# Projection weights loaded one chunk earlier, and the experts' input centred right behind its squares

## The chip, the core and the metric

The kernel runs on one NeuronCore of a Trainium2 chip. Its engines work side by side, each in the order of its own program: TensorE (PE; PEld is its weight load), VectorE (DVE), ScalarE (ACT), GpSimd (POOL) and SyncE (SP), which issues most of the transfers (DMA). The metric is device time in microseconds (us) of one execution; less is better.

## What is computed

One layer of a transformer block for 1024 tokens of width 1024 (with 256 context tokens), all in float32: layer norm and modulation, an input projection, two attentions (a latent one, `y_mla`, and a neighbourhood one, `y_na`), their merge, a second norm, and a mixture of 16 experts in which each expert picks its 128 tokens. The change lies in the merge and in what stands between the two norms:

```python
def _merge(y_mla, y_na, gates, w_proj_mla, w_proj_na, w_out):
    g_mla, g_na = jnp.split(gates, 2, axis=-1)
    return (jax.nn.sigmoid(g_mla) * (y_mla @ w_proj_mla) + jax.nn.sigmoid(g_na) * (y_na @ w_proj_na)) @ w_out

def _layer(...):
    ...
    mix = _merge(y_mla, y_na, gates, lp['w_proj_mla'], lp['w_proj_na'], lp['w_out'])
    x_new = _layer_norm(ALPHA * x + g1 * mix, lp['ln1_g'], lp['ln1_b'])
    u2 = _layer_norm(x_new) * (1 + sc2) + sh2
    moe = _expert_choice_ffn(u2, lp['w_router'], lp['w_exp_gate'], lp['w_exp_up'], lp['w_exp_down'])
    x_new = _layer_norm(ALPHA * x_new + g2 * moe, lp['ln2_g'], lp['ln2_b'])
```

The experts choose tokens by the softmax of `u2 @ w_router`, and `u2` is also what they are fed with.

## The kernel before

The order of the work is written out by hand: each engine runs its instructions in the order in which the program emits them, and waits are put in where data or buffers demand them. Float32 matmuls are done in three passes: `split` gives a tensor a high part (ACT, line 86) and a low part (DVE, line 87), and `mm3` multiplies high by high, high by low and low by high (lines 90 to 92).

The **output projections** run in the pool `pj`. `yT` holds both attentions' results, split into `yhl`. The projection's output columns come in 8 chunks of 128 (`m`); each chunk runs twice, for two halves `b` of the tokens, 24 matmuls of 512 columns each time. `wload(m)` asks for the chunk's weights on the SP queue into `raw` (two buffers) and splits them at once into `hl` (two buffers); in the loop it is called for chunk m+1 at the start of chunk m. Behind the matmuls of (m, b), `gates` multiplies the PSUM result by the gates `sg` (DVE, line 1158) and adds the two attentions into `mix` (line 1161). The PSUM tiles (two, of 1024 columns) are used in turn, so the matmuls of (m+1, b) need `gates` of (m, b). At a chunk's end `wos_load(m+1)` loads 128 rows of w_out on SP and multiplies them by `g1b` on DVE (line 1138), and `small[m]` loads some small tensors. So on DVE each chunk emits: the low part of the next chunk's weights, `gates` for b = 0, `gates` for b = 1, the row of w_out. The pairs of `sg` are loaded on SP two halves ahead, into three buffers. Chunk 0's weights are split ahead of the loop, in two halves, between the splits of `yT`; chunk 1's are split behind the splits of (b, s) = (1, 1).

The **router stage** takes the tokens in 8 blocks of 128. In step t, `main(t)` multiplies block t of `mix` by w_out (48 matmuls, line 1238, in two column halves b of 8 contraction chunks kt), and the dictionary `between` puts other work between its matmuls, mostly on block t-1: `route` transposes the normalised block (line 1309) and ACT copies it to `uT` (line 1310), `logits` multiplies it by the router's weights (line 1317), and `softmax` collects and normalises them (lines 1324, 1337 to 1347). `half(t, b)` adds the residual (line 1248) and takes statistics (line 1249). At the end of a step `norms(t)` normalises the block: line 1264 subtracts the mean and multiplies by the gain, POOL computes the reciprocal deviation `lr` (line 99), line 1277 (1269 in block 7) finishes it by halves, and ACT sums the squares about the new mean into the buffer `u2` (line 1280). Then `pre_mix(t+2)` splits the next but one block of `mix` at the start of step t+1. `norms2(t)` turns the block into the experts' input on DVE: line 1296 centres and scales it into `u2`, line 1298 multiplies by the deviation and shifts. It is emitted in step t+1 behind `softmax`, at (b, kt) = (1, 4), and so ahead of `half(t+1, 1)`. Block 7 has no next step: it is routed and finished behind the loop. Loads of expert weights (`load_next`) are issued on SP in some of the steps into a ring of 17 buffers, and the experts follow.

Of the kernel before, what the change touches and what calls it, by code (L numbers as in the profile page):

```python
# [9 lines left out]
F32 = mybir.dt.float32  # L10
# [17 lines left out]
def block_kernel(ctx, tc, a, out, dbg=None):  # L28
# [56 lines left out]
    def split(hi, lo, src, eng=nc.vector):  # L85
        nc.scalar.activation(hi, src, AF.Copy)  # L86
        eng.tensor_tensor(lo, src, hi.bitcast(F32), op=OP.subtract)  # L87
# [922 lines left out]
    with ExitStack() as st:  # L1010
        p = pool(st, "pj")

        def wload(m):
            raw = p.tile([128, 8, 128], F32, name="raw", bufs=2)
            nc.sync.dma_start(raw, a["w_proj"][m])
            hi, lo = hl_parts()
            if m:
                split(hi, lo, raw)
            return (hi, lo, raw) if m == 0 else (hi, lo)

        hi, lo, raw = wload(0)
        nxt = [(hi, lo)]
        yhl = {}
        for b in range(2):
            cols = slice(b * 512, (b + 1) * 512)
            for s in (1, 0):
                if b == 0:
                    ks = slice(4 * s, 4 * s + 4)
                    split(hi[:, ks], lo[:, ks], raw[:, ks])
                if (b, s) == (1, 0):  # L1030
                    last.pop()()
                    banks(2, 1024, 2, 2)
                yhl[s, b] = big_tile(), big_tile()
                for k in range(4):
                    c = 4 * s + k
                    split(yhl[s, b][0][:, k], yhl[s, b][1][:, k], yT[:, c, cols])
                if (b, s) == (1, 1):
                    nxt.append(wload(1))
        if "ym" in dbg:
            nc.sync.dma_start(dbg["ym"], yT[:, 0:4])  # L1040

# [99 lines left out]
        for m in range(8):  # L1141
            hi, lo = nxt.pop(0)
            if 0 < m < 7:
                nxt.append(wload(m + 1))
            for b in range(2):
                cols = slice(b * 512, (b + 1) * 512)
                sg = sgs.pop(0)
                if 2 * m + b + 2 < 16:
                    sgs.append(sg_load(2 * m + b + 2))
                pt = ps_S()  # L1150
                for s in (1, 0):
                    for kt in range(4):
                        k = 4 * s + kt
                        mm3(pt[:, s * 512:(s + 1) * 512], hi[:, k], lo[:, k], yhl[s, b][0][:, kt], yhl[s, b][1][:, kt], kt == 0, kt == 3)

                def gates(m=m, b=b, pt=pt, sg=sg):
                    t = w1p.tile([128, 2, 512], F32, name="t", bufs=2)
                    nc.vector.tensor_tensor(t, pt.rearrange("p (s c) -> p s c", s=2), sg, op=OP.mult)  # L1158
                    for i in range(2):
                        c = slice(i * 256, (i + 1) * 256)  # L1160
                        nc.vector.tensor_tensor(mix[2 * b + i][:, m], t[:, 0, c], t[:, 1, c], op=OP.add)
                if (m, b) == (7, 1):
                    last.append(gates)
                else:
                    gates()
                if (m, b) == (7, 0):
                    for piece in pre_mix(0, 2):
                        piece()
                    wo_split(0, 0)
                    wo_split(0, 1)  # L1170
            if m < 7:
                wos_load(m + 1)
            small[m]()
# [47 lines left out]
    with ExitStack() as st:  # L1221
# [39 lines left out]
        def norms(t):  # L1261
            xt = xts[t]
            mv, r = aggregate(sts.pop(t))
            nc.vector.scalar_tensor_tensor(xt, xt, mv[:, 0:1], l1g, op0=OP.subtract, op1=OP.mult)
            u2s[t] = p.tile([128, D], F32, name="u2", bufs=2)
            if t == 7:
                st = p.tile([128, 2, 6], F32, name="st2", bufs=1)
                for b, c in enumerate((H0, H1)):
                    nc.vector.scalar_tensor_tensor(xt[:, c], xt[:, c], r[:, 0:1], l1b[:, c], op0=OP.mult, op1=OP.add)
                for b, c in enumerate((H0, H1)):  # L1270
                    nc.vector.bn_stats(st[:, b], xt[:, c])
                mv2[t] = aggregate(st)
                compare(5, 7, 0, 6, nc.gpsimd)
                return
            sm = p.tile([128, 4], F32, name="sums", bufs=3)
            for b, c in enumerate((H0, H1)):
                nc.vector.scalar_tensor_tensor(xt[:, c], xt[:, c], r[:, 0:1], l1b[:, c], op0=OP.mult, op1=OP.add,
                                               accum_out=sm[:, b:b + 1])
            nc.vector.tensor_scalar(sm[:, 2:3], sm[:, 0:1], sm[:, 1:2], 1.0 / D, op0=OP.add, op1=OP.mult)
            nc.scalar.activation(u2s[t], xt, AF.Square, scale=-1.0, bias=sm[:, 2:3], accum_out=sm[:, 3:4])  # L1280
            mv2[t], spread2[t] = (sm[:, 2:3], None), sm[:, 3:4]
# [119 lines left out]
        rowload(l1b, a["ln1_b"])  # L1401
        chunks = {0: 2, 1: 2, 3: 1, 5: 1, 7: 1}
        for t in range(8):
            if t < 7:
                pre_mix(t + 1)[0]()
                pre_x(t + 1)
            for _ in range(chunks.get(t, 0)):
                load_next()
            ps = ps_S(), ps_S()
            between = {(1, 1): lambda: half(t, ps, 0)}  # L1410
            if t == 0:
                between[0, 6] = constants
            else:
                between[0, 7] = lambda: route(t - 1, 0)
                between[1, 0] = lambda: route(t - 1, 1)
                between[0, 4] = lambda: deviation(t - 1)
                between[1, 2] = lambda: logits(t - 1)
                between[1, 4] = lambda: (softmax(t - 1), norms2(t - 1))
            if t >= 2:
                between[0, 3] = lambda: store(t - 2, nc.scalar)  # L1420
            if t == 7:
                rows = hl_tile()
                brow, tok = rows[:, :T], rows[:, T:]
                nc.sync.dma_start(tok, a["tokrow"])
                between[0, 1] = lambda: spread(0, 6)
                between[0, 5] = between[0, 6] = load_next
                between[1, 4] = lambda: softmax(t - 1)
                between[1, 5] = lambda: norms2(t - 1)
                between[1, 3] = lambda: [compare(j, 6) for j in range(3)]
                between[1, 6] = load_next  # L1430
                masks = hl_tile().bitcast(BF16).rearrange("p (i c) -> p i c", i=4)
                masks = [masks[:, i] for i in range(4)]
            main(t, ps, between)
            if t == 7:
                while pos[0] < RB - 2:
                    load_next()
            half(t, ps, 1)
            norms(t)
# [519 lines left out]
```

## Time and profile before

| | us |
|---|---|
| median of 3 timed runs | 1803.76 (1801.29 to 1804.3) |
| the profiled execution | 1792.52 |
| its span, first to last instruction | 1790.7 |
| PE busy | 1676.3 (94%) |
| DVE busy | 1174.9 (66%) |
| ACT busy | 928.5 (52%) |
| POOL busy | 591.8 (33%) |
| mean granted TensorE clock | 0.981 of full speed |

All times below are us from the span's start. The output projections run from about 924 to 1025, the router stage from 1026 to about 1165, the experts from there to the end. In a row of the timeline, the bracket at the end says how long the engine stood idle before that instruction and what ended the wait. SPq is the issue of a transfer on SP's queue, not the transfer. A matmul's duration reaches past the start of the next one, since they are pipelined.

### The profile page before, as it was taken

What the parts mean: (1) busy time and instruction counts of PE and PEld (TensorE: products, weight loads), DVE (VectorE), ACT (ScalarE), POOL (GpSimd) and SP (SyncE); (2) the same over time, 40 slices, a digit from 0 to 9 for tenths busy, and PEclk for the clock granted to TensorE, in tenths of its full rate; (3) what the DMA queues carried; (4) which work ended last, traced back from release to release, by engine and by line L of the source; (5) the groups of instructions that cost most, each with busy time, mean ns of one, the idle gap of its engine ahead of it and who ended that gap; (6) DMA issues with size and microseconds to landing.
All of it is one profiled execution on the core that took longest, in us unless ns stands there. A gap on an engine that the chain in (4) does not pass through costs nothing. (4 is left out here: it accounts for less than half of the span.)

```text
span 1790.7 us, 25352 instructions
## 1 busy us (share of the span) xinstructions
PE 1676.3 (94%) x9609; PEld 1337.7 (75%) x9609; DVE 1174.9 (66%) x1860; ACT 928.5 (52%) x1477; POOL 591.8 (33%) x488
## 2 busy tenths in 40 slices
PE   5999998999999999999988999788999999999995
PEld 3778787897877778888867776556878887888872
DVE  5612251203377766766564577887999999999985
ACT  3422222112366667776660222245777777777764
POOL 0334555542144423222000111256334333433135
PEclk8999999999999999999999999899999999999998
DMA  8334646245244311010026444878999999999944
GB/s 329 113 111 144 224 155 205 83 127 155 81 88 89 75 47 41 21 30 12 1 89 201 164 165 153 328 293 291 366 378 381 392 389 367 384 389 392 361 158 188
DMA packets 96890, 356.62 MB, mean 199 GB/s; under 512 B 28368, under 2 KB 36944, under 8 KB 70912
## 3 DMA queue, kind: packets, MB, share of 16 engines
q1 hardware_dynamic: 78032, 285.78, 44.1%
q0 software_dynamic: 11376, 41.42, 7.7%
q10 hardware_dynamic: 7360, 27.81, 4.0%
q8 instruction: 75, 1.23, 0.3%
q14 instruction: 47, 0.39, 0.1%
HBM read 312.85 MB, written 42.12 MB: 198 GB/s over the span
## 5 line engine op out<-in xcount | busy, mean ns | idle before, releaser
L1712 DVE TENSOR_TENSOR hl<-raw,hl 128x1024 fp32r<-128x1024 f32 x177 | 214.5, 1238 | 21.8 <-ACT hl L1711 19.9
L1711 ACT ACTIVATE hl<-raw 128x1024 fp32r<-128x1024 f32 x182 | 187.9, 1057 | 39.6 <-PE pgate L92 19.0
L405 PE MATMUL pS<-uhi,whi 128*128 128x512 f32 (+1 forms) x440 | 131.0, 386 | 2.4 <-DVE stg L492 1.8
L1608 POOL TENSOR_SCALAR oh<-iot,slot 128x128 bf16<-128x128 f32 x112 | 133.0, 1202 | 0.5
L87 DVE TENSOR_TENSOR wlo<-raw,whi 128x1024 fp32r<-128x1024 f32 x25 | 36.5, 1463 | 143.0 <-ACT whi L86 142.9
L405 PE MATMUL pS<-ulo,whi 128*128 128x512 f32 (+1 forms) x440 | 129.1, 382 | 0.0
L405 PE MATMUL pS<-uhi,wlo 128*128 128x512 f32 (+1 forms) x440 | 128.9, 382 | 0.0
L310 POOL TENSOR_TENSOR sb<-qs,sa 128x512 fp32r<-128x512 f32 x28 | 35.9, 1282 | 255.1 <-DVE sa L309 133.8
L1711 ACT ACTIVATE whl<-raw 128x1024 fp32r<-128x1024 f32 x91 | 96.5, 1060 | 39.5 <-PE pgate L92 19.4
L1865 POOL DMA_INDIRECT acc_d<-ye,idx x15 | 35.1, 2341 | 243.5 <-DVE ye L1859 243.5
L1712 DVE TENSOR_TENSOR whl<-raw,whl 128x1024 fp32r<-128x1024 f32 x88 | 108.4, 1232 | 9.2 <-ACT whl L1711 8.1
L1712 DVE TENSOR_TENSOR raw<-raw 128x1024 fp32r<-128x1024 f32 x89 | 108.8, 1222 | 6.2 <-ACT raw L1711 6.2
L1711 ACT ACTIVATE raw<-raw 128x1024 fp32r<-128x1024 f32 x91 | 96.3, 1058 | 19.7 <-PE pup L92 7.2
L380 POOL TENSOR_TENSOR rawm<-rawm,scol 128x1024 f32<-128x1024 f32 x32 | 63.0, 1969 | 127.9 <-DMA rawm<-in_w_mod_dram 127.9
L1238 PE MATMUL pS<-raw,hl 128*128 128x512 f32 x384 | 96.1, 399 | 2.0 <-DVE t L1158 1.1
L886 DVE TENSOR_REDUCE sn<-pS 128x1 f32<-128x1024 f32 x64 | 78.3, 1223 | 27.4 <-PE pS L92 26.7
L405 PEld LDWEIGHTS pS<-uhi,whi 128*128 128x128 f32 x440 | 79.0, 189 | 22.6 <-issue 4.3
L405 PEld LDWEIGHTS pS<-ulo,whi 128*128 128x128 f32 x440 | 80.2, 188 | 16.4
L405 PEld LDWEIGHTS pS<-uhi,wlo 128*128 128x128 f32 x440 | 80.2, 188 | 16.3
L911 ACT ACTIVATE pt<-pT 128x512 f32<-128x512 f32 x128 | 69.5, 595 | 34.3 <-PE pT L900 31.0
L1238 PEld LDWEIGHTS pS<-raw,hl 128*128 128x128 f32 x384 | 69.7, 188 | 17.6 <-ACT cb L1330 1.5
L900 PE MATMUL pT<-ident,pm 128*128 128x128 f32 x542 | 72.2, 273 | 1.3 <-ACT pt L911 1.3
(493 smaller groups left out, 4683.0 us busy)
## 6 DMA issues: line engine op xcount, KB each, us to landing
raw<-in_w_exp_gate_dram SPq DMA_DIRECT2D x64, 1024.0 KB
raw<-in_w_exp_up_dram SPq DMA_DIRECT2D x64, 1024.0 KB
raw<-in_w_exp_down_dram SPq DMA_DIRECT2D x64, 1024.0 KB
rawm<-in_w_mod_dram POOLq DMA_DIRECT2D x32, 512.0 KB, 3.9
raw<-in_w_in_dram SPq DMA_DIRECT2D x25, 512.0 KB
wm<-in_w_mod_dram SPq DMA_DIRECT2D x8, 1024.0 KB
sig_d<-stg ACTq DMA_DIRECT2D x16, 512.0 KB
sg<-sig_d SPq DMA_DIRECT2D x32, 256.0 KB
```

What stands on the lines that cost most here:

```text
L87: eng.tensor_tensor(lo, src, hi.bitcast(F32), op=OP.subtract)
L310: lo_engine[0].tensor_tensor(lo[:, cs], src[p0:p1, cs], hi[p0:p1, cs].bitcast(F32), op=OP.subtract)
L380: nc.gpsimd.tensor_tensor(raw, raw, scol[:, :, 0:1].to_broadcast([128, KT, 128]), op=OP.mult)
L405: nc.tensor.matmul(pt[:, c0:c1], ww[:, kt], uu[:, kt, c0:c1], start=(kt == 0 and k == 0), stop=(kt == KT - 1 and k == 2))
L886: nc.vector.tensor_reduce(sm[:, 0:1], ps, axis=AX.X, op=OP.max)
L900: nc.tensor.transpose(tb[b][:, (k - k0) * 128:(k - k0 + 1) * 128], Pm[n][:, k * 128:(k + 1) * 128], ident)
L911: nc.scalar.activation(dst, src, AF.Copy)
L1238: nc.tensor.matmul(ps[b], x[:, kt], w[:, kt % 4], start=(kt == 0 and k == 0), stop=(kt == 7 and k == 2))
L1608: nc.gpsimd.tensor_scalar(ohb[:, t], iot, slot[:, t, e:e + 1], None, op0=OP.is_equal)
L1711: nc.scalar.activation(w[:, 0], src, AF.Copy)
L1712: lo_on(e, i).tensor_tensor(w[:, 1], src, w[:, 0].bitcast(F32), op=OP.subtract)
L1865: nc.gpsimd.indirect_dma_start(out=acc_d[:, :], out_offset=bass.IndirectOffsetOnAxis(ap=idx[:, :1], axis=0), in_=ye, in_offset=None, compu ...
```

## The change

In the projections, asking for weights and splitting them are now two functions. `wload()` asks for the next chunk's weights on SP, `wsplit(m)` splits those of chunk m. Two chunks are asked for ahead of everything, the third behind the split of chunk 1, and the one of chunk m+2 at the start of chunk m, just ahead of the split of chunk m+1. The buffers are the same two. In the router stage the two operations of `norms2(t-1)` are taken apart: the first is emitted at the very start of step t, ahead of `pre_mix(t+1)`, the second stays where both stood. In block 7 the subtraction of `norms` is done by halves, each directly ahead of its own half of the next operation. No arithmetic is added or left out.

```diff
-        def wload(m):
-            raw = p.tile([128, 8, 128], F32, name="raw", bufs=2)
-            nc.sync.dma_start(raw, a["w_proj"][m])
+        wraw = []
+
+        def wload():
+            m = len(wraw)
+            if m < 8:
+                wraw.append(p.tile([128, 8, 128], F32, name="raw", bufs=2))
+                nc.sync.dma_start(wraw[m], a["w_proj"][m])
+
+        def wsplit(m):
             hi, lo = hl_parts()
-            if m:
-                split(hi, lo, raw)
-            return (hi, lo, raw) if m == 0 else (hi, lo)
-
-        hi, lo, raw = wload(0)
+            split(hi, lo, wraw[m])
+            return hi, lo
+
+        for _ in range(2):
+            wload()
+        raw = wraw[0]
+        hi, lo = hl_parts()
...
                 if (b, s) == (1, 1):
-                    nxt.append(wload(1))
+                    nxt.append(wsplit(1))
+                    wload()
...
             if 0 < m < 7:
-                nxt.append(wload(m + 1))
+                wload()
+                nxt.append(wsplit(m + 1))
...
             mv, r = aggregate(sts.pop(t))
-            nc.vector.scalar_tensor_tensor(xt, xt, mv[:, 0:1], l1g, op0=OP.subtract, op1=OP.mult)
             u2s[t] = p.tile([128, D], F32, name="u2", bufs=2)
             if t == 7:
                 st = p.tile([128, 2, 6], F32, name="st2", bufs=1)
                 for b, c in enumerate((H0, H1)):
+                    nc.vector.scalar_tensor_tensor(xt[:, c], xt[:, c], mv[:, 0:1], l1g[:, c], op0=OP.subtract, op1=OP.mult)
                     nc.vector.scalar_tensor_tensor(xt[:, c], xt[:, c], r[:, 0:1], l1b[:, c], op0=OP.mult, op1=OP.add)
...
+            nc.vector.scalar_tensor_tensor(xt, xt, mv[:, 0:1], l1g, op0=OP.subtract, op1=OP.mult)
...
         for t in range(8):
+            if t:
+                norms2(t - 1, 0)
...
-                between[1, 4] = lambda: (softmax(t - 1), norms2(t - 1))
+                between[1, 4] = lambda: (softmax(t - 1), norms2(t - 1, 1))
...
-                between[1, 5] = lambda: norms2(t - 1)
+                between[1, 5] = lambda: norms2(t - 1, 1)
```

The SP queue at the head of the projections, before. `raw` is a chunk's weights, `g1b` the gain of w_out, `sg` the gates; the brackets name what the issue waits for:

```order
L1015 DMA raw_8647<-in_w_proj_dram 128x1024 [waits PE_49,Activation_49,Pool_49]
L1015 DMA raw_8684<-in_w_proj_dram 128x1024
L993 DMA g1b_8740<-mod_d_65 128x1024 [waits DVE_49,Activation_49,Pool_49]
L1087 DMA sg_8743<-sig_d_59 128x512 [waits DMAHW7_49,DVE_49,Activation_49]
L1088 DMA sg_8743<-sig_d_59 128x512 [waits DMAHW0_49]
L1087 DMA sg_8746<-sig_d_59 128x512 [waits DMAHW1_49,DVE_49,PE_49]
L1088 DMA sg_8746<-sig_d_59 128x512 [waits DMAHW2_49]
L1137 DMA wos_8742<-in_w_out_dram 128x1024 [waits DMAHW3_49,Activation_49]
```

and now:

```order
L1019 DMA raw_8647<-in_w_proj_dram 128x1024 [waits PE_49,Activation_49,Pool_49]
L1019 DMA raw_8649<-in_w_proj_dram 128x1024
L1019 DMA raw_8689<-in_w_proj_dram 128x1024 [waits DMAHW4_49,DVE_49]
L993 DMA g1b_8742<-mod_d_65 128x1024 [waits DMAHW7_49,Pool_49]
L1096 DMA sg_8745<-sig_d_59 128x512 [waits DMAHW0_49]
L1097 DMA sg_8745<-sig_d_59 128x512 [waits DMAHW1_49]
L1096 DMA sg_8748<-sig_d_59 128x512 [waits DMAHW2_49,PE_49]
L1097 DMA sg_8748<-sig_d_59 128x512 [waits DMAHW3_49]
L1146 DMA wos_8744<-in_w_out_dram 128x1024
```

The third load of weights now stands ahead of `g1b` and of all that follows on SP, and it waits for DVE, which must have split the first chunk out of the buffer that both use.

The DVE in router step 2, from behind block 1's norms to the residual of block 2's second half, before (`hl` is the split of `mix`, `u_...` the experts' input, `lt` the logits):

```order
L87 TENSOR_TENSOR hl<-raw,hl 128x1024
L1287 TENSOR_SCALAR v_9601<-sums 128x1
L1248 SCALAR_TENSOR_TENSOR xt<-xt,pS 128x512
L1249 BN_STATS st<-xt 128x6
L1337 SCALAR_TENSOR_TENSOR lt<-cb,sums,pY 128x16
L1338 SCALAR_TENSOR_TENSOR lt<-lt,r_9603,cb 128x16
L1339 TENSOR_REDUCE sm<-lt 128x1
L1346 RECIPROCAL sm<-sm 128x1
L1347 TENSOR_SCALAR vals<-ex,sm 128x16
L1296 SCALAR_TENSOR_TENSOR u_9574<-xt,sums,sc2b 128x1024
L1298 SCALAR_TENSOR_TENSOR u_9574<-u_9574,r_9603,sh2b 128x1024
L1248 SCALAR_TENSOR_TENSOR xt<-xt,pS 128x512
```

and now:

```order
L1307 SCALAR_TENSOR_TENSOR u_9573<-xt,sums,sc2b 128x1024
L87 TENSOR_TENSOR hl<-raw,hl 128x1024
L1298 TENSOR_SCALAR v_9602<-sums 128x1
L1258 SCALAR_TENSOR_TENSOR xt<-xt,pS 128x512
L1259 BN_STATS st<-xt 128x6
L1348 SCALAR_TENSOR_TENSOR lt<-cb,sums,pY 128x16
L1349 SCALAR_TENSOR_TENSOR lt<-lt,r_9604,cb 128x16
L1350 TENSOR_REDUCE sm<-lt 128x1
L1357 RECIPROCAL sm<-sm 128x1
L1358 TENSOR_SCALAR vals<-ex,sm 128x16
L1309 SCALAR_TENSOR_TENSOR u_9573<-u_9573,r_9604,sh2b 128x1024
L1258 SCALAR_TENSOR_TENSOR xt<-xt,pS 128x512
```

The first of the two operations on `u_...` has moved from behind the softmax to ahead of the split of `mix`; the second alone is left ahead of the residual of the second half.

The DVE on block 7, behind the loop's last matmuls, now. Before, line 1264 did the first operation at full width, 1024 columns, ahead of both halves of the second:

```order
L1263 BN_AGGR mv<-st 128x2
L97 TENSOR_SCALAR lv<-mv 128x1
L1278 SCALAR_TENSOR_TENSOR xt<-xt,mv,ye 128x512
L1279 SCALAR_TENSOR_TENSOR xt<-xt,lr,l1b 128x512
L1278 SCALAR_TENSOR_TENSOR xt<-xt,mv,ye 128x512
L1279 SCALAR_TENSOR_TENSOR xt<-xt,lr,l1b 128x512
L1281 BN_STATS st_10315<-xt 128x6 x2
```

The first operation on the second half of the columns now stands behind the second operation on the first half.

## Rows read from the trace of the kernel before

**Rows 1.** Busy by stretch: us, PE PEld DVE ACT POOL, PEclk, DMA share, GB/s.

```profile
937.96:1014.71 76.75, 68.56 (x289) 54.76 (x289) 37.77 (x49) 6.99 (x7) 10.43 (x15) 0.98 0.59 190
...
1060.52:1075.21 14.69, 13.31 (x78) 10.17 (x76) 10.58 (x21) 3.84 (x9) 2.00 (x2) 1.00 0.30 109
...
1320.00:1360.00 40.00, 40.00 (x188) 32.02 (x187) 37.76 (x40) 31.54 (x35) 14.09 (x11) 1.00 1.00 389
...
912.60:918.80 6.20, 4.36 (x36) 3.11 (x36) 2.28 (x9) 4.39 (x10) 0.00 (x0) 1.00 0.93 336
...
923.20:929.20 6.00, 5.11 (x20) 3.68 (x21) 5.96 (x10) 6.00 (x13) 0.00 (x0) 1.00 0.74 261
```

**Rows 2.** The timeline, PE, around the second chunk of the projections.

```profile
951.57 0.47 PE L90 MATMUL pS<-raw,hl 128*128 128x512 f32 x1 [2.42 <-DVE t L1158]
...
952.34 0.39 PE L90 MATMUL pS<-raw,hl 128*128 128x512 f32 x1
...
962.31 0.39 PE L92 MATMUL pS<-raw,hl 128*128 128x512 f32 x1
```

**Rows 3.** The timeline, ACT and DVE, over the same chunk.

```profile
947.97 1.06 ACT L86 ACTIVATE hl<-raw 128x1024 fp32r<-128x1024 f32 x1 [14.08 <-DMA raw<-in_w_proj_dram]
...
949.06 1.23 DVE L87 TENSOR_TENSOR hl<-raw,hl 128x1024 fp32r<-128x1024 f32 x1 [3.65 <-ACT hl L86]
...
950.21 1.22 DVE L1158 TENSOR_TENSOR t<-pS,sg 128x1024 f32<-128x1024 f32 x1
...
957.61 1.22 DVE L1138 TENSOR_TENSOR wos<-wos,g1b 128x1024 f32<-128x1024 f32 x1 [3.46 <-DMA wos<-in_w_out_dram]
```

**Rows 4.** The timeline, PE, in router step 3.

```profile
1073.70 0.63 PE L1309 MATMUL pT<-ident,xt 128*128 128x128 f32 x4 [0.93 <-DVE xt L1277]
...
1077.23 0.91 PE L1317 MATMUL pY<-uT,wr 128*32 128x128 f32 x16 [0.38 <-ACT uT L1310]
```

**Rows 5.** Timeline, DVE and ACT, router steps 2, 3, then DVE, step 7.

```profile
1066.80 1.28 DVE L1296 SCALAR_TENSOR_TENSOR u<-xt,sums,sc2b 128x1024 f32<-128x1024 f32 x1
...
1068.12 1.28 DVE L1298 SCALAR_TENSOR_TENSOR u<-u,r,sh2b 128x1024 f32<-128x1024 f32 x1
...
1069.32 0.68 DVE L1248 SCALAR_TENSOR_TENSOR xt<-xt,pS 128x512 f32<-128x512 f32 x1
...
1074.51 1.15 ACT L1280 ACTIVATE u<-xt,sums 128x1024 f32<-128x1024 f32 x1 [8.09 <-DVE sums L1279]
...
1076.73 1.23 DVE L87 TENSOR_TENSOR hl<-raw,hl 128x1024 fp32r<-128x1024 f32 x1 [2.26 <-ACT hl L86]
...
1079.90 0.23 DVE L1337 SCALAR_TENSOR_TENSOR lt<-cb,sums,pY 128x16 f32<-128x16 f32 x1 [0.55 <-PE pY L1324]
...
1134.53 0.15 DVE L1287 TENSOR_SCALAR v<-sums 128x1 f32<-128x1 f32 x1 [1.31 <-ACT u L1280]
```

**Rows 6.** The timeline, SP's queue and DVE, head of the projections.

```profile
911.80 0.83 SPq L1015 DMA_DIRECT2D raw<-in_w_proj_dram  x2
...
926.26 0.68 DVE L87 TENSOR_TENSOR hl<-raw,hl 128x512 fp32r<-128x512 f32 x1
...
935.56 1.21 DVE L1138 TENSOR_TENSOR wos<-wos,g1b 128x1024 f32<-128x1024 f32 x1
...
952.29 0.44 SPq L1137 DMA_DIRECT2D wos<-in_w_out_dram  x1
```

**Rows 7.** The timeline, DVE and PE, from chunk 7 into the router stage.

```profile
1022.59 1.22 DVE L1158 TENSOR_TENSOR t<-pS,sg 128x1024 f32<-128x1024 f32 x1
...
1034.10 10.48 PE L1238 MATMUL pS<-raw,hl 128*128 128x512 f32 x45 [1.14 <-DVE t L1158]
```

**Rows 8.** The timeline, DVE and PE, block 7 behind the loop.

```profile
1146.30 1.42 DVE L1269 SCALAR_TENSOR_TENSOR xt<-xt,lr,l1b 128x512 f32<-128x512 f32 x2 [0.44 <-POOL lr L99]
...
1147.20 1.94 PE L1309 MATMUL pT<-ident,xt 128*128 128x128 f32 x8 [4.65 <-DVE xt L1269]
```

**Rows 9.** Waits in the projections: who, for whom: total, times, longest.

```profile
DVE wos L1138 <- DMA wos<-in_w_out_dram: 26.6, 7, 4.3
```


## The prediction

> **What bounds the kernel now.** I read the page first. TensorE (PE) is busy 94% of the span, so most of the time has no pause to take out. Then the busy time by stretch. In the experts, 1320 to 1360 us for one stretch of many, PE is busy without a break at the full clock while DMA moves 389 GB/s [rows 1]. The two stretches that the change touches are different.
>
> *Output projections, chunks 1 to 6.* They take 76.75 us, and PE is busy for only 68.56 of them [rows 1]. Inside a chunk matmuls start 0.2266 us apart: 44 of them between 952.34 and 962.31 [rows 2]. So the 6 x 48 = 288 matmuls need 65.3 us, and 11.5 us are lost. The timeline says where. The matmul at 951.57 is the first of a chunk; PE had stood idle for 2.42 us before it, until VectorE (DVE) line 1158 [rows 2]. That instruction multiplies the first half's result by the gates and so frees the PSUM bank. It could have run long before, since its 24 matmuls, the first of them at 937.96, had ended near 943.7. But DVE takes its work in order, and the low part of the next chunk's weights (line 87, 949.06) stands ahead of it. That one waits for ScalarE (ACT) at 947.97, and ACT for the weights' transfer, which was asked for only one chunk before [rows 3]. So a transfer that PE does not yet need holds up PE through DVE's order.
>
> *Router stage.* Step t projects 128 tokens and, in between, routes token block t-1. It takes 14.69 us [rows 1]. PE waits 0.93 us for DVE line 1277 (the normalised block that it is to transpose) and 0.38 us for ACT line 1310 (the copy of the transposes) [rows 4]. Line 1277 is late because the second half's residual (line 1248 at 1069.32) comes on DVE behind the two full-width operations of `norms2` (1066.80 and 1068.12). Meanwhile DVE had stood idle 2.26 us earlier in the same step, at 1076.73, behind ACT's squares [rows 5].
>
> **The change part by part.**
>
> *Weights one chunk sooner: a gain of 11.5 us.* At the top of chunk m the weights of chunk m+1 have now landed in the chunk before. ACT splits them as soon as chunk m-1's matmuls release the buffer. On DVE the row of w_out (line 1138) still comes first, then the split, then the gates. With its input there the split follows line 1138 directly, and what paces line 1138 is that SP asks for its row only behind the gates of the chunk before. That loop is: gates' end at 951.43, w_out asked for at 952.29 (0.86), used at 957.61 (5.32), then 1.15 to the split, 1.15 to the gates, 1.22 for the gates [rows 3, 6]. That is 9.70 us. PE needs 48 x 0.2266 = 10.88, so PE sets the pace and the pauses go. What is late next is the row of w_out, with 1.2 us to spare.
>
> *Chunk 7 and the way into the router stage: 2.2 us.* From 1014.71 to 1034.10 it takes 19.39 us now. In chunk 7 the gates of the first half start at 1022.59, 7.9 us into the chunk, since the last row of w_out came late too; with that row asked for half a chunk earlier they start when their 24 matmuls end, 23 x 0.2266 + 0.39 + 0.1 = 5.7 us in. From there to PE's first matmul of the second half at 1034.10 it is 11.51 us of DVE work in unbroken order [rows 7]. New: 5.7 + 11.5 = 17.2.
>
> *The price: the SyncE (SP) queue waits earlier, -1.0 us.* The third weight tile shares the first one's buffer, so its load waits on SP until DVE has split the first, at 926.26 + 0.68 = 926.95 us. Behind it stand the loads of `g1b`, two pairs of `sg`, the first row of w_out and a third pair. `g1b` is asked for right behind the two weight tiles of 911.80 now; it goes to about 927.4. DVE wants `g1b` and w_out at 935.56 [rows 6]. Five tiles of 0.524 MB must land by then. Two bursts of the kernel before give the bounds. One (two weight tiles, `g1b`, a pair) was asked for from 911.80, began to flow some 0.8 us later and moved at 336 GB/s; the other (a pair, w_out, a pair) moved at 261 GB/s [rows 1, 6]. At the first rate the five tiles are there at 927.0 + 0.8 + 7.8 = 935.6 (nothing lost), at the second at 937.9 (2.4 us lost). The first three of them are of the fast burst's kinds, the last two of the slow one's: 0.8 + 4.7 + 4.0 makes 936.5, and 1.0 us lost. DVE stands there before the gates of chunk 0, so PE's chunk 1 starts that much later; nothing gives it back.
>
> The Trainium skill speaks against this part here, on its page "DMA: Bandwidth & Descriptors", section "Anatomy of one DMA": a semaphore is waited for by the issuing sequencer, so one waiting load holds all loads behind it. The same section puts a transfer at about 2.0 us plus its bytes over 436 GB/s; as an estimate, five tiles would be there 8.0 us after 927.0, at 935.0, and the price would be nil, the sum 1.0 us better. The two bursts of this trace moved more slowly than that, so they decide.
>
> *`norms2`'s first operation right behind the squares: 7.7 us.* 1.32 us of DVE work (1066.80 to 1068.12) leaves the way to line 1248 and goes into the idle 2.26 us. There it runs after ACT's squares (1074.51 plus 1.15 and 0.19 for reading the sum), so it ends at about 1077.1 and the split of the mix behind it starts 0.3 to 0.4 us later than now [rows 5]. Its cover is the wait for `collect` before line 1337, 0.55 us; if that is gone, `lt` is late by the rest. New loop by the rows: 2.79 from `lt` to line 1248, 5.19 on to the squares, 2.72 to the logits, 2.67 to the next `lt`: 13.37 us, as much as PE's own work (14.69 - 0.93 - 0.38 = 13.38) [rows 4, 5]. So both waits go and nothing new binds, with hardly a margin. Step 2 gains 0.92 (its logits wait belongs to step 1, where nothing is earlier yet), steps 3 to 6 gain 1.28 each, the logits of step 6 another 0.38: 6.4 us. In step 6 line 1248 runs 1.3 us earlier on top, and block 6's squares are 7.7 us earlier than now. Step 7 is DVE's alone from its first instruction behind those squares (1134.53) to its last; there the moved operation only changes its place, so 7.7 passes through.
>
> *Block 7 centred by halves: -0.4 us.* Now one full-width subtraction (1.28) runs while POOL works out `lr`, and then two halves follow at 1146.30 (1.42 for both). In the new order DVE waits for `lr` after half a subtraction and does the other 0.68 us after it. The first half is ready as before, the second 0.68 later. The 8 transposes start at 1147.20 and the second four need it only 1 us in, so some 0.3 of it is hidden [rows 8]. Bounds: 0 and 0.7.
>
> *What follows.* The expert stage starts that much earlier with the same requests released by the same instructions, and PE is busy in all of the stretch shown [rows 1]: the shift reaches the end whole.
>
> **Sum:** 11.5 + 2.2 - 1.0 + 7.7 - 0.4 = 20.0 us. The profiled execution took 1792.5 (span 1790.7), so 1772.5 for one like it. The median shown is 1803.76, 11.2 above the profiled one; no row says why. I take the same 20.0 off it: **1783.8**. Bounds of the terms: price 0 to 2.4, last block 0 to 0.7, and half-clock stretches such as the one that leaves the mean at 0.98 in [rows 1], which may be more in other runs and go with the pauses: 1778 to 1787.
>
> **The rivals.**
>
> *The row of w_out becomes the bound.* If with the other traffic it takes 7.5 us instead of 5.32, the loop is 11.9 and six chunks lose 6 us again: 1789.8. For it: DVE waits for that transfer in every chunk (7 waits, 26.6 us [rows 9]). Against: the longest wait is 4.3 us where the one of my loop is 3.46 [rows 3, 9], which makes the longest landing 6.2 and that loop 10.6, still under 10.88. 13%.
>
> *The moved operation only fills DVE.* If line 1337 comes 0.6 us late in each step, about half of the router's 7.3 is left: 1787.4. For it: the margins above are near nil. Against: DVE is busy 10.58 us of a step [rows 1]. 8%.
>
> *The experts give it back.* DMA moves 389 GB/s without a pause there [rows 1]; if the weights' stream is what really sets the end and it starts only half as much earlier, 10 us stay: 1793.8. Against: PE has no pause there that a late transfer could have made. 5%.
>
> *Nothing moves:* PE's pauses stay, because the gates stand behind w_out as they stood behind the weights: 1803. 2%.
>
> *Slower.* The same row of w_out at the head of DVE, but taking 11 us: the loop is 15.4, against the 12.8 that a chunk takes now, so the projections lose 15.5; chunk 7's 2.2 goes, and the price of 1.0 and the router's 7.3 remain: 9.2 us more, 1813. It decides from a landing of 9.5 us on, where a chunk of 13.8 has eaten the other terms. 2%.
>
> **How the numbers follow.** Forecast 70% (1778 to 1787). To hold the time 8 times in 10 the range goes up over the first two rivals and one us down: 1777 to 1791. A measurement of this kernel tells about 0.2%, 3.6 us, from no change. Faster 0.96 (forecast and the first three rivals), same 0.02, slower 0.02.
>
> **What would show it.** Right: PE starts chunk 7 about 65.5 us after chunk 1 and has no pause over 0.3 us in between; line 87 no longer stands between w_out and a late gate; `g1b` is asked for near 927.4; router steps of 13.4 us without a wait at the transposes; the second four transposes of block 7 half a us later. Wrong: pauses in the projections ended by w_out's transfer, steps over 13.8 us, DMA waits among the experts, or chunk 1 starting over 2.5 us later than now.

## The result, and the profile after

| | before | after |
|---|---|---|
| median on record | 1804.03 us (4 runs, 1801.29 to 1804.55) | 1775.85 us (4 runs, 1770.9 to 1776.61) |
| a second series of runs | 1797.93 (21 runs, 1786.67 to 1803.15) | 1773.4 (6 runs, 1768.3 to 1781.09) |
| span of the first and of a second profiled execution | 1790.7, 1796.1 | 1774.8, 1773.1 |

The ratio on record is 0.9866, with a 95% interval of 0.9832 to 0.9900; in the second series it is 0.9879 (0.9845 to 0.9913). The change is faster: by some 22 to 24 us by these ratios, by 28.2 and 24.5 us by the medians. The forecast was 1783.8 us (1777 to 1791), 20.0 us off a median of 1803.76. So the direction held. The measured median, 1775.85, lies 1.2 us under the lower end of the range; the ratio, taken off the same 1803.76, gives 1779.6, inside it.

The stages first, by busy time in the kernel after (columns as in [rows 1]: length, then PE, PEld, DVE, ACT, POOL, PEclk, DMA share, GB/s). The first line is projection chunks 1 to 6, the second a router step:

```profile
939.72:1005.13 65.41, 65.41 (x288) 54.18 (x289) 38.25 (x50) 5.32 (x5) 9.94 (x15) 1.00 0.69 225
1045.97:1059.41 13.44, 13.14 (x76) 10.27 (x75) 10.56 (x22) 3.84 (x8) 2.01 (x2) 1.00 0.33 119
```

Six chunks take 65.41 us with PE busy in all of them, at the full clock; before they took 76.75, of which 68.56 busy, at a mean clock of 0.98 [rows 1]. A router step takes 13.44 us instead of 14.69.

The timeline of the kernel after at the head of the projections (SP's queue, DVE, PE), then in a router step, then at block 7:

```profile
912.36 15.50 SPq L1019 DMA_DIRECT2D raw<-in_w_proj_dram  x3
927.96 0.38 SPq L993 DMA_DIRECT2D g1b<-mod_d  x1
937.31 1.23 DVE L1147 TENSOR_TENSOR wos<-wos,g1b 128x1024 f32<-128x1024 f32 x1 [1.11 <-DMA wos<-in_w_out_dram]
939.72 0.50 PE L90 MATMUL pS<-raw,hl 128*128 128x512 f32 x1 [2.50 <-DVE t L1168]
...
1048.03 1.28 DVE L1307 SCALAR_TENSOR_TENSOR u<-xt,sums,sc2b 128x1024 f32<-128x1024 f32 x1 [1.31 <-ACT u L1291]
1059.56 0.60 PE L1320 MATMUL pT<-ident,xt 128*128 128x128 f32 x4
...
1125.35 0.92 POOL L99 TENSOR_TENSOR lr<-lv,mhalf 128x1 f32<-128x1 f32 x1 [8.12 <-DVE lv L97]
1128.65 1.09 PE L1320 MATMUL pT<-ident,xt 128*128 128x128 f32 x4 [0.41 <-DVE xt L1279]
1130.28 0.55 POOL L99 TENSOR_TENSOR lr<-lv,mhalf 128x1 f32<-128x1 f32 x1 [4.01 <-DVE lv L97]
```

The row of the three loads of weights lasts 15.50 us, since the third of them waits on SP; `g1b` is asked for at 927.96 instead of behind the two loads of 911.80, and DVE stands 1.11 us before the first row of w_out [rows 6]. The moved operation (L1307) starts right behind ACT's squares, and the transposes that waited 0.93 us [rows 4] wait no more. The second four transposes of block 7 wait 0.41 us.

Stage lengths, each the difference of two row starts, but for the end of the last stage. A: PE's first projection matmul; B: DVE's first row of w_out; C: the gates of (7,1); D, E, F: the first, seventh and eighth `lt`; G: `idx`, expert 0's list of tokens, by which POOL gathers them; H: PE's transpose of `top`, the highest affinities that DVE picks out next for the other experts; End: the end of PE's last instruction. C to D is 17.8 us in all four.

| us | A-B | B-C | D-E | E-F | F-G | G-H | H-End |
|---|---|---|---|---|---|---|---|
| before, first trace | 11.77 | 97.18 | 88.21 | 12.79 | 11.06 | 28.01 | 584.28 |
| before, second trace | 11.78 | 98.78 | 88.19 | 12.79 | 10.83 | 33.65 | 584.91 |
| after, first trace | 12.97 | 83.61 | 81.88 | 11.53 | 11.06 | 31.65 | 584.21 |
| after, second trace | 12.85 | 85.23 | 81.91 | 11.54 | 10.28 | 29.68 | 584.26 |
| mean change | +1.1 | -13.6 | -6.3 | -1.3 | -0.3 | -0.2 | -0.4 |
| forecast | +1.0 | -13.7 | -6.4 | -0.9 | 0 | 0 | 0 |

Up to G the stages together are 20.3 us shorter in the mean, against a forecast of 20.0. From B to C each kernel differs by 1.6 us between its two executions. In the second trace of after this is a stretch of half clock at the start of chunk 1 (columns as above):

```profile
939.03:943.01 3.98, 3.98 (x10) 3.12 (x11) 2.64 (x5) 0.00 (x0) 0.00 (x0) 0.57 0.64 145
```

The granted clock was 0.57 there, behind a pause of PE of 1.86 us, and most matmuls started 0.427 us apart instead of 0.2266. In the first trace of after chunk 1 stands behind a longer pause, 2.50 us, and no such stretch follows. The chunks behind it run without a pause in both traces. From G to H each kernel differs from one execution to the next by more than in any other stage. The experiments are mostly about that place, where the first trace of after lost 3.6 us against the first of before, and the second trace of before 5.6 us.

### The profile page after: what moved, and what is told of

The parts are those of the page before. It is cut to its first block, busy times and chain, and to the rows that moved or that the text cites. A ratio compares the mean times of both kernels' runs of the same rounds, so it can differ in the third digit from the quotient of the medians.

```text
span 1774.8 us, 25355 instructions
## 1 busy us (share of the span) xinstructions
PE 1672.5 (94%) x9609; PEld 1338.5 (75%) x9609; DVE 1174.4 (66%) x1861; ACT 929.4 (52%) x1477; POOL 593.7 (33%) x488
## 4 chain that ended last, share of the span: by engine, by line
PE 69%; DVE 9%; DMA 6%; POOL 6%; ACT 5%; issue 3%; SPq 0%; ACTq 0%; POOLq 0%; DVEq 0%
PE pS L405 10%; PE pY L923 4%; DMA rawm<-in_w_mod_dram 4%; PE pT L900 3%; PE pgate L90 3%; PE pS L90 3%; PE pD L90 3%; PE pS L92 3%; PE pD L92 3%; PE pD L91 3%; PE pup L90 3%; PE pS L91 3%; PE pgate L92 3%; PE pup L91 3%; PE pup L92 3%
```

## The experiments

Every run was timed in rounds beside the kernel before; ratios are to those runs.

**Both kernels again.** No edit.

> The kernel before, unchanged, to see why its profiled execution (1792.5 us) was 11.2 us below the median of its runs. If executions of one kernel scatter by what a single place does, the new trace shows that place: all steps up to the gather of expert 0 as in the first trace (gather issued at 1163.0 +- 1 us from the span's start) and the difference behind it, or a lower granted clock in one stretch. If the first trace comes from a chip that is faster as a whole, every stage is longer by the same 0.6%. Time: 1801 to 1805 in both cases.

Measured: median 1799.07 (12 runs, 1790.21 to 1805.81), ratio 1.0012 (0.9990 to 1.0034). One kernel spreads over 16 us. The new trace reaches `idx` 0.9 us sooner than the first one and PE's transpose of `top` 4.7 us later. Its timeline there (DVE, POOL, PE):

```profile
1163.21 7.02 DVE L1477 TENSOR_TENSOR gg<-picked 128x1 f32<-128x1 f32 x1
1163.25 2.36 POOL L1712 TENSOR_TENSOR whl<-raw,whl 128x1024 fp32r<-128x1024 f32 x1
1165.56 4.64 POOL L1712 TENSOR_TENSOR hl<-raw,hl 128x1024 fp32r<-128x1024 f32 x2
1170.15 0.68 DVE L1525 MAX8 top<-oh 32x8 f32<-32x512 f32 x1
1195.33 0.28 PE L1536 MATMUL pT<-ident,top 32*128 32x32 f32 x1 [5.28 <-DVE top L1525]
```

The same rows in the first trace of the kernel before:

```profile
1164.12 0.16 DVE L1477 TENSOR_TENSOR gg<-picked 128x1 f32<-128x1 f32 x1
1164.30 2.36 POOL L1712 TENSOR_TENSOR whl<-raw,whl 128x1024 fp32r<-128x1024 f32 x1 [0.18 <-ACT whl L1711]
1190.60 0.25 PE L1536 MATMUL pT<-ident,top 32*128 32x32 f32 x1
```

`gg`, the sum of two 128x1 columns that hold the gates of expert 0, takes 0.16 us when POOL's first weight split starts 0.18 behind it, and 7.02 when it starts 0.04 behind it: it ends with POOL's third split, at 1170.20. DVE's search for the highest affinities (`top`) stands behind it, and PE finds it 5.28 us late. So the first expectation, one place that scatters, held; the chip-wide 0.6% fell. With 5.6 us this place accounts for half of the 11.2 us between the first profiled execution and the median; the other half stays open.

> The changed kernel, unchanged, on the chip of the runs beside it, for a second trace. If the loss at the gather of expert 0 is a property of the kernel, the gather again takes about 8 us from issue to the transposes and block 7's store again ends behind the index; if it was a chance of that one execution, the transposes start 4.8 to 5.3 us after the index and the span is about 4 us shorter (1771).

Measured: median 1773.4 (6 runs), ratio 0.9879. The loss at the gather came again, smaller, between what the two expectations said: 6.61 us from issue to transposes, where the first trace had 8.15.

**`gg` with one operand**, on the kernel before:

```diff
-            nc.vector.tensor_tensor(dst, picked[:, i:i + 1], picked[:, i + 1:i + 2], op=OP.add)
+            if i:
+                nc.vector.tensor_reduce(dst, picked[:, i:i + 2], axis=AX.X, op=OP.add)
+            else:
+                nc.vector.tensor_tensor(dst, picked[:, i:i + 1], picked[:, i + 1:i + 2], op=OP.add)
```

> The kernel before with one instruction replaced: the sum of expert 0's gates (gg, two columns of picked) is a reduction of one operand instead of an addition of two; same arithmetic. In the trace of before_again this 128x1 addition took 7.02 us instead of 0.16, from 0.04 us ahead of POOL's first weight split to the end of POOL's third, and PE met the delay at the transposes of top (5.28 us). Theory that DVE's second input and POOL share a port: gg takes 0.2 us or less in this trace, PE waits under 0.5 us at the transposes of top, the median is 2 to 5 us under that of the kernel before and the highest runs (1803 to 1806) become rare. Rival, that DVE was held by something else (its semaphores, the transfers): gg again long in about half of the traces, median equal within 1 us.

Measured: median 1792.71 (11 runs, 1789.91 to 1796.7) against 1798.54, ratio 0.9975 (0.9956 to 0.9995). Nothing is left above 1797, where the 15 runs of the kernel before beside it reach 1805.55. Its timeline:

```profile
1162.81 0.15 DVE L1478 TENSOR_REDUCE gg<-picked 128x1 f32<-128x2 f32 x1
1162.85 2.37 POOL L1715 TENSOR_TENSOR whl<-raw,whl 128x1024 fp32r<-128x1024 f32 x1
1188.83 0.25 PE L1539 MATMUL pT<-ident,top 32*128 32x32 f32 x1
```

POOL starts 0.04 us behind `gg`, as in the bad execution, and `gg` takes 0.15. Over all 14 traces: with two operands and POOL 0.04 behind, `gg` was held in 4 of 4 (7.02 three times, 2.42 once, until POOL's first split ended); with POOL 0.18 or more behind, in 0 of 6; with one operand and POOL 0.04 behind, in 0 of 3 (in the fourth with one operand POOL came later). The Trainium skill states the cause on its page "SBUF — State Buffer", section "Who interferes with whom": a DVE instruction with two inputs in SBUF shares the second read interface with a GpSimd instruction that reads SBUF, and the one issued second waits until the first has ended. The traces agree on which form waits. They differ in two things: the wait lasted over three POOL instructions, 7.02 us, not one of 2.36, in three of the four; and the instruction that was held is, by the trace, the one that started first, by 0.04 us.

**One part alone.** The weights one chunk sooner, with the rest as before; then the moved operation alone, with block 7 by full width (the diffs are the parts of the change).

> Only the weights asked for one chunk sooner; norms2 and block 7 as before. The forecast's terms make 11.5 + 2.2 - 1.0 = 12.7 us less than the kernel before (ratio 0.9930). In the trace: no pause of PE between chunk 1 and chunk 7, the gates of (7,1) 12.4 to 13 us sooner, router steps of 14.7 us as before. If the part of the gain that was lost at the gather of expert 0 in the changed kernel belongs to this part, the time is only 8 to 9 us less, with the gather landing 8 us after its issue instead of 4.8.

> Only the first operation of norms2 moved behind the squares; weights as before, block 7 by full width as before. The forecast's term is 7.7 us less than the kernel before (ratio 0.9957): steps of 13.4 instead of 14.7 us, the logits of block 7 7.5 to 7.9 us sooner. If the shift is lost at the gather of expert 0 (the landing 8 us instead of 4.8), 3.5 to 4.5 us less. If the moved operation only fills DVE (rival of the prediction), 3.6 us less and steps of 14.1.

Measured: weights alone 1781.22 (7 runs), ratio 0.9917 (0.9888 to 0.9947); router alone 1786.85 (9 runs), ratio 0.9942 (0.9919 to 0.9966). Both gained more than their terms in time (about 15 and 10 us for 12.7 and 7.7), but not in their stages. Weights alone: A to C 98.06 us, 10.9 and 12.5 less than in the two traces of before, with 1.6 us lost at half clock in chunk 1 as in the second trace of after. Its trace has a `gg` of 7.02 us and belongs to a run of 1789.63; one other run took 1791.02, and five lie at 1777.85 to 1781.37. Router alone: D to E 81.94 and E to F 11.46, together 7.6 less; its `gg` took 0.16, with POOL 0.74 behind it. That the rest of the gain is a `gg` that is held less often is likely by how the runs fall into groups, but not shown: each kernel has one trace. The two traces also tell which part turns the order at the gather: with the weights alone it follows `idx` by 0.45 us and PE has the rows 4.69 us later; with the router part alone it is 0.67 and 5.26. The full-width block 7 of router alone also prices the halves: 11.46 against 11.53 us, 0.07.

**The split behind the gates**, on the kernel before: the transfer where it was, only DVE's and ACT's split moved.

```diff
             if 0 < m < 7:
-                nxt.append(wload(m + 1))
+                raw = p.tile([128, 8, 128], F32, name="raw", bufs=2)
+                nc.sync.dma_start(raw, a["w_proj"][m + 1])
...
                     gates()
+                if b == 0 and 0 < m < 7:
+                    nxt.append(hl_parts())
+                    split(*nxt[-1], raw)
```

> The kernel before, with the next chunk's weights asked for where they were, but split behind the gates of the first half instead of ahead of them, from chunk 1 on; nothing else changed. Theory of the prediction, that it is DVE's order and not the transfer that stops PE: by the rows of before the low part is ready some 10.2 us into a chunk of 10.88, so the pauses go without an earlier load and without the later g1b: from the first row of w_out to the gates of (7,1) 85 to 88 us on DVE instead of 97 to 99, the first row of w_out 11.8 us behind PE's first projection matmul as before, time 10 to 13 us under the kernel before. Rival, that the weights' transfer is the bound: PE waits for the low part at each chunk's start instead, 2 us or more, and 0 to 5 us are gained.

Measured: B to C 87.7 us, 1785.12 (7 runs), ratio 0.9919 (0.9888 to 0.9950), with a `gg` of 7.02 in its trace. After the first matmul of chunk 1, PE pauses only where chunk 2 begins:

```profile
954.27 0.50 PE L90 MATMUL pS<-raw,hl 128*128 128x512 f32 x1 [1.30 <-ACT hl L86]
955.53 0.50 PE L92 MATMUL pS<-raw,hl 128*128 128x512 f32 x1 [0.53 <-DVE hl L87]
```

So the pauses of the kernel before were made by the split's place on DVE. With the transfer at its old place all but one of them go, and the first row of w_out is not late (A to B 11.77).

**Every row of w_out but the first loaded twice**, on the kernel after.

```diff
             nc.sync.dma_start(wos[:, m], a["w_out"][m * 128:(m + 1) * 128])
+            if m:
+                nc.sync.dma_start(wos[:, m], a["w_out"][m * 128:(m + 1) * 128])
```

> The changed kernel with every row of w_out but the first loaded twice, the second transfer behind the landing of the first. It prices the loop that the prediction found next (gates' end, issue, landing, 1.15 to the gates: 9.70 us, 5.32 of it the landing). Theory: the second landing adds 2.5 to 5.3 us to the loop, which makes 12.2 to 15.0 us a chunk instead of 10.88 or less; seven rows, so 9 to 29 us more than the changed kernel, with DVE waiting for the transfer ahead of every gates of a first half. If the row has more room than that loop says, under 3 us more.

Measured: 1791.13 (9 runs), 16.9 us over the kernel after with one operand, timed beside it; B to C is 102.71 us, against 83.64 there. The shortest turn of the loop that holds all its parts (DVE, PE, SP):

```profile
951.95 1.22 DVE L1170 TENSOR_TENSOR t<-pS,sg 128x1024 f32<-128x1024 f32 x1
953.31 0.47 PE L90 MATMUL pS<-raw,hl 128*128 128x512 f32 x1 [3.61 <-DVE t L1170]
954.03 0.43 SPq L1146 DMA_DIRECT2D wos<-in_w_out_dram  x1
958.63 0.33 SPq L1148 DMA_DIRECT2D wos<-in_w_out_dram  x1
962.09 1.23 DVE L1149 TENSOR_TENSOR wos<-wos,g1b 128x1024 f32<-128x1024 f32 x1 [6.21 <-DMA wos<-in_w_out_dram]
964.37 1.22 DVE L1170 TENSOR_TENSOR t<-pS,sg 128x1024 f32<-128x1024 f32 x1
```

From gates to gates this turn is 12.42 us, and PE stops for 3.61 again. Its landings take 4.60 and 3.46 us instead of one of 5.32, and 9.70 + 2.74 is 12.44. The six turns up to chunk 6 take 12.42 to 14.70 us with landings of 8.06 to 10.33 together, each 4.4 more than its landings, as in the prediction's loop (9.70 - 5.32). So that loop is right. Its spare time shows in the first trace of after itself: until the gates of the first halves have caught up with PE, they follow each other in 9.45 to 10.51 us (chunks 0 to 5), 0.4 to 1.4 less than the 10.88 that PE needs.

**What holds up expert 0.** The chain of waits of the kernel after runs through two transfers, block 7's store and the gather (start, us, what):

```profile
1134.50 9.68 DMA acc_d<-xt
1144.18 8.01 DMA xe<-u_d,idx
1152.33 1.09 PE pY L1656 x4
```

Its timeline (DVE, POOL, SP, PE) shows the order behind it:

```profile
1143.19 0.16 DVE L1490 TENSOR_TENSOR idx<-picked 128x1 int32<-128x1 f32 x1
1144.18 1.09 POOL L1495 DMA_INDIRECT xe<-u_d,idx  x1 [6.81 <-DVE uT L1488]
1144.84 0.33 SPq L1228 DMA_DIRECT2D raw<-in_w_exp_up_dram  x1
1152.33 1.09 PE L1656 MATMUL pY<-ident,xe 128*128 128x128 f32 x4 [9.08 <-DMA xe<-u_d,idx]
```

The first of three 1 MB loads is asked for 1.65 us behind `idx`, in this and in the first trace of before (1164.23 - 1162.58). The gather follows `idx` by 0.45 us there and by 0.99 here, because the store had not landed: so the chain has it, though the row's own bracket names a DVE operation. So the loads come 0.66 us behind the gather instead of 1.19. A load of weights now stands nearer ahead of the store. These are the last such load and the store, before and then after:

```profile
1143.15 0.33 SPq L1218 DMA_DIRECT2D raw<-in_w_exp_gate_dram  x1
1153.90 0.50 SPq L1259 DMA_DIRECT2D acc_d<-xt  x1
```

```profile
1127.59 0.33 SPq L1228 DMA_DIRECT2D raw<-in_w_exp_gate_dram  x1
1134.50 0.44 SPq L1269 DMA_DIRECT2D acc_d<-xt  x1
```

That is 10.75 us ahead and now 6.91; with the weights alone it is 11.43, with the router part alone 6.79. So the nearer load comes from the shorter router steps. Whether it makes the store late is what the first of two edits asks; the second moves the loads behind the gather:

```diff
-                while pos[0] < RB - 2:
+                while pos[0] < RB - 4:
...
         store(7, nc.sync)
+        while pos[0] < RB - 2:
+            load_next()
```

> The changed kernel with the last two expert-weight loads of step 7 issued on SP behind block 7's store instead of ahead of it. In the changed kernel the store, issued at 1134.12 and 1134.50, ended at 1144.18, behind weights that keep DMA at over 400 GB/s to 1139, and the gather of expert 0 and ACT's first weight split waited for it. Theory that the store is what is late: it ends 3 to 5 us earlier, the gather is issued 0.45 us behind idx instead of 0.99, ACT's split starts 0.4 us behind idx. Then POOL's first split comes within 0.2 us of gg, and by the port theory gg takes 7 us in some executions: time between 1772 and 1779, no gain that can be relied on. Rival, that only the three loads behind the gather matter: gather and time as in the changed kernel (1773 to 1776).

```diff
-        load_next()
-        load_next()
-        load_next()
...
         xT = [transposed(xe0, "x", h, True) for h in range(2)]
+        for _ in range(4):
+            load_next(nc.scalar)
```

(with the load inside the first weight splits held back to the same place.)

> The changed kernel with the four expert-weight loads that follow the gather of expert 0 on SP (three of them 0.66 to 1.63 us behind it) issued by ACT behind the copies of expert 0's transposes. Theory that these 1 MB loads hold up the gather: from issue to PE's transposes 4 to 5 us instead of 6.6 to 8.1, tau0's transposes of top 2 to 3.5 us earlier behind idx, time 2 to 3 us under the changed kernel. Rival, that block 7's store alone holds it up: 6.6 to 8.1 us from issue to transposes as before, time equal, or up to 1.5 us more for ACT's issues.

Measured, the gather's issue and the transposes in the kernel with the store ahead, then in the one with the loads behind (its first load goes out at 1150.69):

```profile
1142.55 1.09 POOL L1497 DMA_INDIRECT xe<-u_d,idx  x1 [6.26 <-DMA raw<-in_w_exp_gate_dram]
1143.74 0.33 SPq L1228 DMA_DIRECT2D raw<-in_w_exp_up_dram  x1
1147.67 1.09 PE L1658 MATMUL pY<-ident,xe 128*128 128x128 f32 x4 [5.51 <-DMA xe<-u_d,idx]
```

```profile
1144.16 1.09 POOL L1495 DMA_INDIRECT xe<-u_d,idx  x1 [5.91 <-DMA acc_d<-xt]
1150.69 0.34 ACTq L1228 DMA_DIRECT2D raw<-in_w_exp_up_dram  x1
1148.70 1.09 PE L1653 MATMUL pY<-ident,xe 128*128 128x128 f32 x4 [5.49 <-DMA xe<-u_d,idx]
```

Both cure it: 5.12 and 4.54 us instead of 8.15. With the store ahead of the last two loads the gather also follows `idx` by 0.45 us again, here and in the two later kernels that have it; in the five traces of the kernel after and its variants without it, it is 0.45 (twice), 0.55, 0.73 and 0.99. So it is the loads ahead of the store that can make it late. From idx to PE's transpose of `top` it is 28.22 and 28.78 us. In time they cannot be told from the kernel after: 1774.15 (1772.15, 1774.15 and 1783.96) and 1772.61 (3 runs each).

**Versions meant to be faster than both.**

> The changed kernel with gg as a reduction of one operand, nothing else. In both traces of the changed kernel POOL's first weight split comes 0.8 to 1.1 us behind gg, since ACT's split waits for block 7's store, so by the port theory it meets the long gg seldom: median within 1.5 us of the changed kernel (1773 to 1776), and its highest runs (1780 to 1781) gone if they were such executions. Rival, that the long gg is as frequent here as in the kernel before: 3 to 6 us under the changed kernel.

> The changed kernel with four edits together: gg as a reduction of one operand, block 7's store ahead of the last two weight loads, the four weight loads behind the transposes, and the third projection weight tile asked for behind the first row of w_out instead of ahead of g1b. By the terms measured so far: 1.2 us at the head of the projections, 0.5 at the gather's issue, 2 to 3 at its landing, and no execution with a gg of 7 us: 3.5 to 5 us under the changed kernel, about 1769. If the edits only move waits to the next transfer, within 1 us of the changed kernel.

> The changed kernel with three edits: gg as a reduction of one operand, block 7's store ahead of the last two weight loads of step 7, the third projection weight tile asked for behind the first row of w_out. The loads behind the gather stay on SP. By the traces so far: 1.1 us at the head, 1.5 to 3.4 us from idx to the transposes of top (28.2 us as in store_ahead instead of 29.7 and 31.7), no execution with a gg of 7 us: 2.5 to 4.5 us under the changed kernel. If not: equal within 1 us.

Measured: 1774.19 (6 runs, 1771.58 to 1775.61), 1774.07 (5 runs, 1768.25 to 1774.69) and 1773.3 (6 runs, 1770.25 to 1775.26). The last one's stages are as expected: A to B is 11.77 us again (a price of 1.1 recovered, of which 0.8 is left at C: A to C is 95.79, against 96.58 in the first trace of after) and `idx` to `top` 27.42, with POOL's split 0.04 behind a `gg` of 0.16. Its span is 1769.8, the shortest of all traces. But its median is only 0.9 under the kernel beside it and 0.1 under the 1773.4 of the kernel after. No version is shown to beat the change. No run of the three lies above 1775.61, where the kernel after had 2 of 10 above 1780; that those two had a held `gg` is likely, but no trace shows one in the kernel after.

## Why the prediction was right, and where not

- **Weights one chunk sooner, chunk 7 and the way on: 11.5 + 2.2.** Right: B to C -13.6 us; between the two first traces 11.3 in the six chunks and 2.2 behind them. The cause was shown by moving the split alone, and the next bound by doubling the row of w_out.
- **The price of SP's queue: 1.0, bounds 0 to 2.4.** Right: 1.0 to 1.2 in each trace with the early third load, 0 in the two where it was put behind w_out. The prediction's estimate from the Trainium skill, page "DMA: Bandwidth & Descriptors", section "Anatomy of one DMA", made it nil; but that section gives its 2.0 us plus bytes over 436 GB/s for transfers that GpSimd issues, and these were issued by SP. The two bursts of [rows 1] were the better guide.
- **`norms2` moved: 6.4 and 1.3.** Right: D to E -6.3, with steps of 13.44 for a forecast of 13.4. From the sixth `lt` to the seventh it stays 14.66 us, where it was 14.77; the prediction had the gain of the steps end with step 6.
- **Block 7 by halves: 0.4.** Mis-sized: 0.07. The second transposes do wait, 0.41 us, but POOL's `lr` took 0.92 us (the row at 1125.35 above) in place of the 1.45 of the kernel before:

```profile
1144.81 1.45 POOL L99 TENSOR_TENSOR lr<-lv,mhalf 128x1 f32<-128x1 f32 x1 [9.50 <-DVE lv L97]
```

- **"What follows: the shift reaches the end whole."** This step failed. The prediction asked whether PE waits in the experts, but not what the shorter router steps do to the transfers that run beside them. Block 7's store ended behind `idx`, where it had ended before it, and expert 0's gather then met loads that follow DVE and not the store. In the two traces of after G to H is 1.7 and 3.6 us longer than in the first trace of before; in a third one, the kernel after with one operand, whose gather went out 0.45 us behind `idx` and took 4.86 to the transposes, only 0.9.
- **"The median shown is 1803.76 [...] no row says why. I take the same 20.0 off it."** This failed too, the other way. The profiled execution had a short `gg`. Most others of the kernel before probably had a held one, as in its second trace: one operand alone moves the median by 5.8 us. In the kernel after, ACT's first split and so POOL's wait for the late store, and POOL came 0.8 to 1.1 us behind `gg` in both traces. So the change takes away a stall that the trace it was judged by did not contain. Counted from the kernel before with one operand: 1792.71 - 20.0 + (0.9 to 3.6) is 1773.6 to 1776.3, and the kernel after lies at 1773.4 and 1775.85.

So the sum of terms was right within half a us up to `idx`, and the absolute time was 8 us too high through its base: 1803.76 lies 11 us over those 1792.71, and the 0.9 to 3.6 us lost at the gather go the other way. Of the 11 us, one operand explains 5.8; the other 5.2, by which the first runs lay over the later median of 1798.54, no run explains. That the two errors partly cancel is luck. The prediction's 0.2% for what a measurement can tell was too small for this kernel too: its runs spread over 16 us. The rivals fell: PE has no pauses by w_out; no step is over 13.8 us but that last one, in which no gain was forecast; and PE's one DMA wait among the later experts, 3.6 and 3.3 us at one gather, was there before (3.5).

Still open: PE's first projection matmul came between 921.5 and 927.6 us over the traces, in code that nothing here touches, and why the first three runs of the kernel before all lay above 1801.

## What to carry to other kernels

Before a sum is taken off a median, find out whether the profiled execution is a typical one: if it is 11 us below the median, profile again and compare stage by stage, since a stall that comes in some executions only may be what the change removes or adds. Where the compute beside a stream of transfers gets shorter, look at the last store and the first gather behind it: their order against the prefetches may turn. By this case, a small DVE operation with two SBUF inputs should not stand just ahead of a row of long POOL instructions; give it a form with one.

## What the hardware showed unexpectedly

- A 128x1 addition on DVE was held for 7.02 us by three POOL instructions in a row, though it stands 0.04 us ahead of the first of them in the trace; a 128x2 reduction at the same place took 0.15.
- It goes the other way too: POOL's 128x1 `lr` takes 0.55 us where it starts 0.03 us ahead of a full-width two-input DVE operation. It takes 0.92 or 1.45 where it starts 0.22 us behind a half or full-width one, and ends 0.4 us after that.
- An indirect gather of 128 rows took 4.5 us to the first use with the 1 MB loads 6.5 us behind it, 4.7 to 5.1 with them 1.2 behind, 5.3 with them 0.98 behind (the router part alone), and 6.6 and 8.1 with them 0.92 and 0.66 behind.
